# Per-head sums of squares from two split products, placed later in the tensor engine's order

## The chip, the cores and the metric

The kernel runs on one core of a Trainium2 chip. A core has five engines with their own instruction streams: TensorE (PE, with its weight loads shown apart as PEld), VectorE (DVE), ScalarE (ACT), GpSimd (POOL) and SyncE (SP), which here issues nearly all DMAs. Engines wait for one another through semaphores. The metric is the device time of one execution in microseconds (us).

## The reference

One step of a decoder trunk: one layer, 2048 prompt positions and 8 sample positions of width 1024 (32-bit floats). What bears on the change is the normalisation of q and k. Each has 12 heads of 64 in three groups of four (g = 0, 1, 2), and every head is divided by its own root mean square before the rotary turn's result is used:

```python
def rmsnorm(x, gain):
    xf = x.astype(jnp.float32)
    y = xf * lax.rsqrt(jnp.mean(xf * xf, axis=-1, keepdims=True) + EPS)
    return (y * gain.astype(jnp.float32)).astype(x.dtype)

def project_inputs(h, pos, w_in, q_norm_g, k_norm_g):
    z = h @ w_in
    u, q, k, v, a_pool, a_attn = jnp.split(z, IN_SPLITS, axis=-1)
    q = rope(rmsnorm(q.reshape(b, l, N_HEADS, HEAD_DIM), q_norm_g), pos)
    k = rope(rmsnorm(k.reshape(b, l, N_HEADS, HEAD_DIM), k_norm_g), pos)
    ...
```

Around it stand the modulated input norm, pooled and gated branches, dilated attention in the three head groups, an output projection, and a feed-forward part of width 4096 with squared relu.

## The kernel before

**Arithmetic.** Large products are made from 32-bit values split in two parts of the type float32r: the high part is a copy into that type (`S.copy`, ACT), the low part the difference (POOL for weights, L184). `mm3` (L156) makes three products of one block: high by high, high by low, low by high. One product of a 128x128 block with 512 columns in float32r is one instruction. `small` (L168) makes a single product of plain 32-bit floats: one instruction with two records, since it appears twice in the trace.

**Stages.** Up to 76 us the conditioning and the first normalised input; 76 to 298 us q, k and v of the first half of the positions (`qkv(0)`); 298 to 760 gates, conditioning and the pooled branch; 760 to 1128 q, k, v of the second half (`qkv(1)`), with batches of the attention (`ps_s`, `ps_t`, `ps_o`) laid between; then the rest of the attention, the output projection and the feed-forward part up to 3065 us. In each `qkv`, the head groups follow as g = 2, 1, 0, in each group q, then k, then v.

**Units.** q and k are made in units of at most 512 positions: 512, 256 and 264 (256 and the 8 sample positions) in `qkv(0)`, 512 and 512 in `qkv(1)`. There are 3 x 2 x 3 = 18 units in the first and 3 x 2 x 2 = 12 in the second, 30 in all: 18 of 512, 6 of 256, 6 of 264 columns. A unit has two halves of the head width (48 products of `ps_qk`). `qk_out` takes them out of PSUM on ACT as `ab` and, squared, as `qsq` (L381, L382). `after_qk` (L391) does the rest: it loads cosines and sines (`cs`, SP L395), adds the two squares on POOL (L396), does the rotary turn on DVE and POOL into `ro` (L400 to L405), and gives up its turn. Later it is called again: one `small` product with a matrix of ones per head (`hones`, part of the constants `cp`) sums the squares over the partitions of each head, into `ps_hs` (L408); ACT takes the root (L410), DVE the reciprocal (L411) and multiplies (L413); ACT and POOL split the result into `ohl` (L435, L436), and SP stores it as `qst` or `kst` (L444, L447).

**What sets the order.** TensorE's order is written out: the class `Order` adds up a model time from a length given with each product, and polls waiting generators after every third product. A generator yields the model time after which it is to go on; `after_qk` yields `HS_AT` there, 6500 model ns after the unit's products. So a greater number puts the `ps_hs` product later among the others. The order of all other engines is the scheduler's, which prefers what is under `first()`. All loads and stores of these stages stand in one queue, SP's, in that order, and one that waits holds those behind it. Weights come by `load_w` (L178), three raw buffers `wr`, one load ahead.

**Buffers.** In `gtp` there is a tag `th` with two buffers of 512 columns of 4 bytes, which `gate` uses from 298 us on.

Of the kernel before, what the change touches and what calls it, by code (L numbers as in the profile page):

```python
# [8 lines left out]
F32 = mybir.dt.float32  # L9
F32R = mybir.dt.float32r  # L10
# [6 lines left out]
P = 128  # L17
# [9 lines left out]
KEEP = (128, 512, 2048)  # L27
NEG = -1.0e30
DEPTH = 1
HS_AT = 6500  # L30
ADA_GAP = 3600
DEPTH_O = 1
R1 = 2
# [16 lines left out]
PERIOD1 = 4200.0  # L50
PERIOD2 = 3600.0
PRIO = 400
CPACK = (("cT", (8, 9)), ("bada", (48,)), ("gn", (2, 8)), ("ident", (128,)), ("ones", (128,)), ("hones", (128,)),
         ("mask", (256,)), ("qkg", (2, 2)), ("psc", (4,)), ("icnt", (4, 16)), ("stT", (4, 8, 15)), ("fold", (9,)),
         ("sel", (16,)), ("par", (2,)))
CPW = sum(int(np.prod(s)) for _, s in CPACK)
# [58 lines left out]
def emit(tc, I, O):  # L115
# [52 lines left out]
    def small(ps, w, x, ns=220.0):  # L168
        mm(ps, w, x, True, True, ns)
# [59 lines left out]
    for name, shape in CPACK:  # L229
# [5 lines left out]
            v = v.rearrange("p (a b c) -> p a b c", a=shape[0], b=shape[1])  # L235
        cv[name] = v
        off += n
    cT, ident, ones, hones, mask = cv["cT"], cv["ident"], cv["ones"], cv["hones"], cv["mask"]
    bada, gn, qkg, icnt, stT = cv["bada"], cv["gn"], cv["qkg"], cv["icnt"], cv["stT"]
    epsc = cst.tile([P, 1], F32, name="epsc")  # L240
    V.memset(epsc, EPS)
    mod = cst.tile([P, 48, 9], F32, name="mod")
# [141 lines left out]
    def qkv(ci, hb, done=None):  # L384
# [6 lines left out]
        def after_qk(g, qk, t0, n, ab, sq):  # L391
# [2 lines left out]
            cs = ap.tile([P, 2, 512], F32, tag="cs", bufs=2 - ci, name="cs")  # L394
            SP.dma_start(out=cs[:, :, :n], in_=I["rope"][:, :, BASE[ci] - 1024 * ci + t0:BASE[ci] - 1024 * ci + t0 + n])  # L395
            G.tensor_tensor(out=sq[:, 0, :n], in0=sq[:, 0, :n], in1=sq[:, 1, :n], op=ALU.add)  # L396
            a, b, co, si = ab[:, 0, :n], ab[:, 1, :n], cs[:, 0, :n], cs[:, 1, :n]
            t = ap.tile([P, 2, 512], F32, tag="rt", bufs=1, name="rt")
            o = ap.tile([P, 2, 512], F32, tag="ro", bufs=2, name="ro")
# [5 lines left out]
            V.tensor_tensor(out=o[:, 1, :n], in0=o[:, 1, :n], in1=t[:, 1, :n], op=ALU.add)  # L405
            yield HS_AT
            pst = stp.tile([P, 512], F32, tag="st", name="ps_hs")
            small(pst[:, :n], hones, sq[:, 0, :n], n / 0.6)  # L408
            rs = ap.tile([P, 512], F32, tag="qrs", bufs=2 - ci, name="qrs")
            S.activation(out=rs[:, :n], in_=pst[:, :n], func=AF.Sqrt, scale=1.0 / 64, bias=epsc)  # L410
            V.reciprocal(out=rs[:, :n], in_=rs[:, :n])  # L411
# [309 lines left out]
    def ada_load(op, b):  # L721
        out = []
        for kk in range(4):
            raw = op.tile([P, 1024], F32, tag="wr", bufs=8, name="wr")
            SP.dma_start(out=raw, in_=I["w_ada"][b, kk])
            out += [raw[:, 0:512], raw[:, 512:1024]]
        return out
# [10 lines left out]
    def opening():  # L738

        ost = ExitStack()  # L740
        op = pool(ost, "open", side="left")
        raws = {0: ada_load(op, 0)}
        x0 = load_x0(op, 0)
        raws[2] = ada_load(op, 2)
        raws[1] = ada_load(op, 1)
        keys = [("w_in", 8 + 6 * qk + i) for qk in range(2) for i in range(2)]
        ws, pss = [weights(*keys[0])], []
        x1 = load_x0(op, 1)
        raws[3] = ada_load(op, 3)
        hxs = hx(h0, KD, 0, 512)  # L750

        def part(t):
            if t:
                ws.append(weights(*keys[t]))
            pss.append(mmp.tile([P, 512], F32, tag="mm", name="ps_qk"))
            mm3(pss[t], wk(ws[t], KD)[:4], hxs[:4], False, stop=False)

        m0 = ada_rows(op, 0, raws[0])
        acc = x_sum(0, 0, x0, V)
        rs0 = rms_finish(npl, stp, acc, HALVES[0][0][2])  # L760
        m0()
        m2 = ada_rows(op, 2, raws[2])
        m2()
        make_h(0, 0, x0, rs0, h0, range(4))
        m1 = ada_rows(op, 1, raws[1])
        acc = x_sum(0, 1, x1, V)
        part(0)
        m1()
        part(1)
        m3 = ada_rows(op, 3, raws[3])  # L770
        rs1 = rms_finish(op, stp, acc, HALVES[0][1][2])
        part(2)
        m3()
        make_h(0, 0, x0, rs0, h0, range(4, KD))
        make_h(0, 1, x1, rs1, h0)
        part(3)
        ost.close()
        return ws, pss
# [689 lines left out]
```

## Time and profile before

| | us |
|---|---|
| median of three runs | 3069.55 |
| lowest, highest | 3059.91, 3071.53 |
| profiled execution, its own time | 3066.39 |
| its span in the trace | 3064.6 |

In that execution the granted TensorE clock was 0.98 of full speed on the mean. Busy shares of the span: PE 96%, PEld 82%, DVE 52%, ACT 32%, POOL 32%. The chain that ended last runs over PE for 76% of the span, over DVE for 5% and over DMAs for 5%. Times in the rows further down are microseconds from the start of the span; the second number of a row in a timeline is how long the group of instructions in it took, and square brackets hold idle time before it and what ended it. A product's record and its end are modelled, so neighbouring records overlap; the distance between starts is the safer number.

### The profile page before, as it was taken

To read this page: it belongs to the slowest core of one execution; us is meant where nothing else is said; L and a number is where in the kernel's file an instruction comes from. 1 tells how busy PE (TensorE), PEld (TensorE's weight loads), DVE (VectorE), ACT (ScalarE), POOL (GpSimd) and SP (SyncE) were. 2 spreads that over 40 slices of the span, in tenths; PEclk is the share of its full clock that TensorE was granted. 3 is DMA by queue.
4 is the path that set the end of the run, shared out by engine and by line. 5 is a ranking of instruction groups with operands and counts; after the bars stand their busy time and mean duration, and the time that the engine had idled before them with its cause. 6 is when DMAs were issued, how large, how long until landed. Compare 5 with 4: busy or idle time off the path is not lost.

```text
span 3064.6 us, 40910 instructions
## 1 busy us (share of the span) xinstructions
PE 2953.0 (96%) x16220; PEld 2516.0 (82%) x16220; DVE 1589.7 (52%) x2645; ACT 983.2 (32%) x1771; POOL 969.5 (32%) x510
## 2 busy tenths in 40 slices
PE   7999999999898789999999999999999999999999
PEld 3899788887788688877899999999877888888887
DVE  4656352541744524447865545555677554444444
ACT  4433342433554434433521221121235211111211
POOL 2666341333533312234532122121245312221221
PEclk8999999999999889999999999999999999999999
DMA  6453852334777779976321111111272211111111
GB/s 239 147 162 133 287 185 95 118 118 147 199 198 209 185 177 233 246 233 224 104 86 42 49 49 49 42 49 48 91 242 83 76 42 56 48 49 42 55 43 69
DMA packets 207599, 379.09 MB, mean 124 GB/s; under 512 B 47424, under 2 KB 103072, under 8 KB 206624
## 3 DMA queue, kind: packets, MB, share of 16 engines
q1 hardware_dynamic: 195888, 359.63, 38.3%
q10 hardware_dynamic: 11520, 16.85, 1.5%
q8 instruction: 128, 2.10, 0.3%
q14 instruction: 63, 0.52, 0.1%
HBM read 294.89 MB, written 81.75 MB: 123 GB/s over the span
## 4 chain that ended last, share of the span: by engine, by line
PE 76%; DVE 5%; DMA 5%; issue 4%; POOL 3%; ACT 2%; SPq 1%; DVEq 0%; ACTq 0%; POOLq 0%
PE ps_dn L153 23%; PE ps_up L153 22%; PE ps_g L153 10%; PE ps_v L153 4%; PE ps_qk L153 4%; PE ps_u L153 3%; PE ps_wo L153 3%; PE ps_o L153 2%; PE ps_pb L153 1%; POOL wh L184 1%; PE ps_s L153 1%; PE ps_ada L153 1%; PE ps_t L172 1%; DMA t1d<-ta 1%; POOL ohl L436 1%
## 5 line engine op out<-in xcount | busy, mean ns | idle before, releaser
L184 POOL TENSOR_TENSOR wh<-wr,wh 128x1024 fp32r<-128x1024 f32 (+1 forms) x274 | 651.0, 2384 | 1676.7 <-ACT wh L183 1668.5
L153 PE MATMUL ps_dn<-rt,wh 128*128 128x512 f32 (+2 forms) x3840 | 727.5, 350 | 5.5 <-POOL wh L184 3.3
L153 PEld LDWEIGHTS ps_dn<-rt,wh 128*128 128x128 f32 x3840 | 619.6, 188 | 108.8 <-POOL wh L184 4.2
L183 ACT CAST wh<-wr 128x1024 fp32r<-128x1024 f32 (+1 forms) x306 | 309.3, 1023 | 735.7 <-issue 562.3
L1293 DVE SCALAR_TENSOR_TENSOR xa<-ps_dn,mod,xa 128x512 f32<-128x512 f32 (+1 forms) x640 | 405.0, 641 | 202.9 <-PE ps_dn L153 201.5
L153 PE MATMUL ps_g<-h,wh 128*128 128x512 f32 (+2 forms) x1920 | 391.5, 355 | 0.4 <-POOL wh L184 0.4
L153 PE MATMUL ps_up<-hb,wh 128*128 128x264 f32 (+2 forms) x2304 | 371.5, 319 | 0.0
L153 PE MATMUL ps_up<-ha,wh 128*128 128x512 f32 x1536 | 365.7, 394 | 0.0
L153 PEld LDWEIGHTS ps_up<-hb,wh 128*128 128x128 f32 x2304 | 332.0, 188 | 36.3
L153 PEld LDWEIGHTS ps_g<-h,wh 128*128 128x128 f32 x1920 | 308.7, 191 | 48.5 <-POOL wh L184 1.0
L153 PEld LDWEIGHTS ps_up<-ha,wh 128*128 128x128 f32 x1536 | 286.7, 188 | 64.6 <-issue 0.5
L153 PE MATMUL ps_qk<-h,wh 128*128 128x512 f32 (+2 forms) x1440 | 301.5, 363 | 8.8 <-POOL h L318 6.5
L1277 DVE TENSOR_TENSOR r<-r 128x512 f32<-128x512 f32 (+2 forms) x160 | 99.2, 620 | 387.5 <-ACT r L1276 387.4
L153 PEld LDWEIGHTS ps_qk<-h,wh 128*128 128x128 f32 x1440 | 234.4, 193 | 51.0 <-POOL h L318 7.7
L1279 DVE TENSOR_TENSOR rt<-r,rt 128x512 fp32r<-128x512 f32 (+2 forms) x160 | 217.9, 1362 | 81.8 <-ACT rt L1278 81.6
L1276 ACT ACTIVATE r<-ps_up 128x512 f32<-128x512 f32 (+2 forms) x160 | 82.2, 514 | 415.1 <-PE ps_up L153 415.1
L153 PE MATMUL ps_v<-wh,h 128*128 128x256 f32 (+1 forms) x1224 | 171.8, 297 | 25.8 <-ACT wh L183 18.9
L153 PEld LDWEIGHTS ps_v<-wh,h 128*128 128x128 f32 (+1 forms) x1224 | 157.7, 195 | 31.1 <-ACT wh L183 19.3
L932 ACT ACTIVATE pe<-pe,ost 128x128 f32<-128x128 f32 (+1 forms) x192 | 87.1, 455 | 142.0 <-DVE ost L930 136.9
L930 DVE CUSTOM_DVE_ANT_0 pe<-ps_s,cp 128x128 f32<-128x128 f32 (+1 forms) x192 | 61.4, 358 | 119.6 <-PE ps_s L153 119.4
L1278 ACT CAST rt<-r 128x512 fp32r<-128x512 f32 (+2 forms) x160 | 85.8, 536 | 66.3 <-DVE r L1277 66.3
L436 POOL TENSOR_TENSOR ohl<-ro,ohl 128x256 fp32r<-128x256 f32 (+1 forms) x66 | 76.7, 1185 | 90.9 <-ACT ohl L435 90.8
(181 smaller groups left out, 3003.7 us busy)
## 6 DMA issues: line engine op xcount, KB each, us to landing
wr<-in_w_up SPq DMA_DIRECT2D x72, 512.0 KB
wr<-in_w_down SPq DMA_DIRECT2D x68, 512.0 KB
wr<-in_w_in SPq DMA_DIRECT2D x64, 512.0 KB
wr<-in_w_ada SPq DMA_DIRECT2D x48, 512.0 KB
slab<-kst SPq DMA_DIRECT2D x40, 512.0 KB
wr<-in_w_out SPq DMA_DIRECT2D x32, 512.0 KB
cs<-in_rope SPq DMA_DIRECT2D x18, 512.0 KB
qst<-ohl SPq DMA_DIRECT2D x9, 1024.0 KB
```

What stands on the lines that cost most here:

```text
L153: PE.matmul(ps, w, x, start=start, stop=stop)
L172: PE.transpose(ps, x, idn)
L183: S.copy(out=wt[:, 0, :n], in_=raw[:, :n])
L184: eng.tensor_tensor(out=wt[:, 1, :n], in0=raw[:, :n], in1=wt[:, 0, :n].bitcast(F32), op=ALU.subtract)
L436: G.tensor_tensor(out=pl, in0=pi, in1=ph.bitcast(F32), op=ALU.subtract)
L930: V.tensor_tensor_reduce(out=pe[:, off:off + nk], in0=ps[:, off:off + nk], in1=mask[:, mo:mo + nk], scale=-0.125, scalar=3.0e38, op0=ALU.a ...
L932: S.activation(out=pe[:, off:off + nk], in_=pe[:, off:off + nk], func=AF.Exp, scale=-1.0, bias=o[:, 64:65], accum_out=o[:, 65:66])
L1276: S.activation(out=r1[:, :l], in_=ps[:, :l], func=AF.Relu)
L1277: V.tensor_tensor(out=r1[:, :l], in0=r1[:, :l], in1=r1[:, :l], op=ALU.mult)
L1278: S.copy(out=rt[:, 0, a:a + l], in_=r1[:, :l])
L1279: V.tensor_tensor(out=rt[:, 1, a:a + l], in0=r1[:, :l], in1=rt[:, 0, a:a + l].bitcast(F32), op=ALU.subtract)
L1293: V.scalar_tensor_tensor(out=x[:, c0 + a:c0 + a + lp], in0=ps[:, :lp], scalar=mod[:, 40 + m, 0:1], in1=x[:, c0 + a:c0 + a + lp], op0=ALU.m ...
```

## The change

The matrix of ones per head leaves the packed constants (1355 to 1227 columns) and is loaded by itself in the opening, into one of the three raw buffers for weights, and copied on ACT to float32r. In each of the 30 units the sum of squares is split: a copy on ACT (`sh`) and a difference on DVE (`sl`), both under `first()`. They lie in the buffers of the tag `th`: a unit of 512 or 264 columns takes both, one of 256 takes one. The single product is replaced by two float32r products, and their model length is about 216 ns each for 512 columns in place of 853 in all. `HS_AT` goes from 6500 to 11000.

```diff
-HS_AT = 6500
+HS_AT = 11000
...
-CPACK = (("cT", (8, 9)), ("bada", (48,)), ("gn", (2, 8)), ("ident", (128,)), ("ones", (128,)), ("hones", (128,)),
+CPACK = (("cT", (8, 9)), ("bada", (48,)), ("gn", (2, 8)), ("ident", (128,)), ("ones", (128,)), 
...
-    cT, ident, ones, hones, mask = cv["cT"], cv["ident"], cv["ones"], cv["hones"], cv["mask"]
+    cT, ident, ones, mask = cv["cT"], cv["ident"], cv["ones"], cv["mask"]
...
+    hones = cst.tile([P, P], F32R, name="hones")
...
             G.tensor_tensor(out=sq[:, 0, :n], in0=sq[:, 0, :n], in1=sq[:, 1, :n], op=ALU.add)
+
+            m = 1 if n > 256 else 2
+            hl = [gtp.tile([P, m, 512 // m], F32R, tag="th", bufs=2, name="sqhl") for _ in range(2 // m)]
+            sh, sl = (hl[0][:, 0, :n], hl[-1][:, m - 1, :n])
+            with first():
+                S.copy(out=sh, in_=sq[:, 0, :n])
+                V.tensor_tensor(out=sl, in0=sq[:, 0, :n], in1=sh.bitcast(F32), op=ALU.subtract)
...
-            small(pst[:, :n], hones, sq[:, 0, :n], n / 0.6)
+            mm(pst[:, :n], hones, sh, True, False, max(107.0, n / 2.4 + 2.5))
+            mm(pst[:, :n], hones, sl, False, True, max(107.0, n / 2.4 + 2.5))
...
         raws[3] = ada_load(op, 3)
+        raw = rawp.tile([P, 1024], F32, tag="wr", name="wr")
+        SP.dma_start(out=raw[:, :P], in_=I["hones"])
+        S.copy(out=hones, in_=raw[:, :P])
```

TensorE in `qkv(0)`, the q units of group g = 1, named A (512), B (256) and C (264) below. Before:

```order
L153 MATMUL ps_qk<-h,wh 128x264 x12
L153 MATMUL ps_hs<-qsq,cp 128x512
L153 MATMUL ps_qk<-h,wh 128x264 x36
L153 MATMUL ps_qk<-h,wh 128x512 x3
L153 MATMUL ps_hs<-qsq,cp 128x256
L153 MATMUL ps_qk<-h,wh 128x512 x27
L153 MATMUL ps_hs<-qsq,cp 128x264
L153 MATMUL ps_qk<-h,wh 128x512 x18
```

And after:

```order
L153 MATMUL ps_qk<-h,wh 128x264 x48
L153 MATMUL ps_qk<-h,wh 128x512 x3
L153 MATMUL ps_hs<-sqhl,hones 128x512 x2
L153 MATMUL ps_qk<-h,wh 128x512 x21
L153 MATMUL ps_hs<-sqhl,hones 128x256 x2
L153 MATMUL ps_qk<-h,wh 128x512 x24
L153 MATMUL ps_hs<-sqhl,hones 128x264 x2
L153 MATMUL ps_qk<-h,wh 128x256 x48
```

Each `ps_hs` stands some 40 products later, and 24 products lie between that of B and that of C where 27 lay before. For the k units it is 45 products of 256 columns (`ps_v`).

DVE at the same place; `qrs` is the root that is inverted. Before:

```order
L404 TENSOR_TENSOR ro<-ro,rt 128x512
L405 TENSOR_TENSOR ro<-ro,rt 128x512
L401 TENSOR_TENSOR ro<-ab,cs 128x256
L403 TENSOR_TENSOR ro<-ab,cs 128x256
L404 TENSOR_TENSOR ro<-ro,rt 128x256
L405 TENSOR_TENSOR ro<-ro,rt 128x256
L411 RECIPROCAL qrs<-qrs 128x512
L413 TENSOR_TENSOR ro<-ro,qrs 128x512 x2
```

And after:

```order
L404 TENSOR_TENSOR sqhl<-qsq,sqhl 128x512
L409 TENSOR_TENSOR ro<-ab,cs 128x256
L411 TENSOR_TENSOR ro<-ab,cs 128x256
L412 TENSOR_TENSOR ro<-ro,rt 128x256
L413 TENSOR_TENSOR ro<-ro,rt 128x256
L404 TENSOR_TENSOR sqhl<-qsq,sqhl 128x256
L420 RECIPROCAL qrs<-qrs 128x512
L404 TENSOR_TENSOR sqhl<-qsq,sqhl 128x264
L422 TENSOR_TENSOR ro<-ro,qrs 128x512 x2
```

The difference of C (264 columns) stands behind the reciprocal of A. On ACT the copies of B and C both stand ahead of A's root, as the rows there after the change show:

```order
L183 CAST wh<-wr 128x1024
L403 CAST sqhl<-qsq 128x256
L403 CAST sqhl<-qsq 128x264
L419 ACTIVATE qrs<-ps_hs,epsc 128x512
L382 ACTIVATE ab<-ps_qk,cp 128x512
L383 ACTIVATE qsq<-ps_qk 128x512
L419 ACTIVATE qrs<-ps_hs,epsc 128x256
```

So A's root waits until C's copy has its buffer.

SP's queue near the end of `qkv(1)`, around the load of the last half of v's weights (`in_w_v`); `kst` there is the store of the first k unit of g = 0, and the `cs` load beside it belongs to the second. Before:

```order
L976 DMA att_79<-ost 128x4x66 x4
L968 DMA vt<-vscr 128x8x256
L395 DMA cs<-in_rope 128x2x512
L447 DMA kst_74<-ohl 512x1x512
L180 DMA wr<-in_w_v 128x1024
L180 DMA wr<-in_w_in 128x1024 x4
```

And after:

```order
L988 DMA att_79<-ost 128x4x66 x3
L456 DMA kst_74<-ohl 512x1x512
L988 DMA att_79<-ost 128x4x66
L980 DMA vt<-vscr 128x8x256
L396 DMA cs<-in_rope 128x2x512
L180 DMA wr<-in_w_v 128x1024
```

The store now stands ahead of the last attention store and of the `vt` load; the weight load is still behind both the store and the `cs` load.

## Rows read from the trace of the kernel before

**Rows 1.** The page's busy times: engine, us, share, instructions.

```profile
PE 2953.0 (96%) x16220; PEld 2516.0 (82%) x16220; DVE 1589.7 (52%) x2645; ACT 983.2 (32%) x1771; POOL 969.5 (32%) x510
```

**Rows 2.** Stretches: start:end, length; busy PE, PEld, DVE, ACT, POOL; granted clock, DMA.

```profile
76.00:150.00 74.00, 67.04 (x471) 62.34 (x471) 48.68 (x71) 31.51 (x61) 42.83 (x39) 0.95 0.44 142
150.00:298.00 148.00, 147.50 (x1033) 135.20 (x1032) 86.35 (x110) 53.46 (x97) 93.00 (x74) 1.00 0.46 150
1055.00:1072.00 17.00, 0.46 (x4) 0.26 (x3) 11.04 (x10) 3.62 (x11) 8.55 (x6) 0.65 0.57 186
1072.00:1084.00 12.00, 10.28 (x45) 9.98 (x46) 1.36 (x9) 2.73 (x10) 4.68 (x2) 0.50 0.62 180
```

**Rows 3.** Waits of PE, 70 to 300 us: total us, times, longest.

```profile
PE ps_hs L153 <- POOL qsq L396: 3.4, 3, 2.5
```

**Rows 4.** Waits of PE, 755 to 1130 us.

```profile
PE ps_v L153 <- ACT wh L183: 18.9, 2, 16.6
PE ps_o L153 <- ACT px L940: 5.7, 2, 3.7
```

**Rows 5.** The tile ps_hs: ns shortest/median/longest, first and last start, forms.

```profile
L153 PE MATMUL ps_hs<-qsq,cp x60: 377/591/697, 88.1 to 1084.8; 128*128 128x512 f32 x36, 128*128 128x256 f32 x12, 128*128 128x264 f32 x12
```

**Rows 6.** Weight loads around a 512-column product: start, us, instruction.

```profile
242.05 0.31 PEld L153 LDWEIGHTS ps_hs<-qsq,cp 128*128 128x128 f32 x2
242.59 0.19 PEld L153 LDWEIGHTS ps_qk<-h,wh 128*128 128x128 f32 x1 [0.24 <-issue]
243.02 0.56 PEld L153 LDWEIGHTS ps_qk<-h,wh 128*128 128x128 f32 x4 [0.24 <-issue]
```

**Rows 7.** Weight loads around a 256-column product.

```profile
105.60 0.30 PEld L153 LDWEIGHTS ps_hs<-qsq,cp 128*128 128x128 f32 x2
105.93 0.76 PEld L153 LDWEIGHTS ps_qk<-h,wh 128*128 128x128 f32 x5
```

**Rows 8.** Long runs of float32r products on PE.

```profile
981.55 8.58 PE L153 MATMUL ps_qk<-h,wh 128*128 128x512 f32 x36
204.97 15.48 PE L153 MATMUL ps_v<-wh,h 128*128 128x256 f32 x129
```

**Rows 9.** PE in the first units, where it waits.

```profile
88.14 1.12 PE L153 MATMUL ps_hs<-qsq,cp 128*128 128x512 f32 x2 [0.60 <-POOL qsq L396]
...
93.96 5.59 PE L153 MATMUL ps_qk<-h,wh 128*128 128x256 f32 x32 [3.86 <-POOL h L318]
...
127.50 0.71 PE L153 MATMUL ps_hs<-qsq,cp 128*128 128x264 f32 x2 [2.49 <-POOL qsq L396]
```

**Rows 10.** DVE in the units of g = 1.

```profile
162.48 1.76 DVE L404 TENSOR_TENSOR ro<-ro,rt 128x512 f32<-128x512 f32 x1 [1.18 <-POOL rt L400]
164.17 0.68 DVE L405 TENSOR_TENSOR ro<-ro,rt 128x512 f32<-128x512 f32 x1
164.77 0.41 DVE L401 TENSOR_TENSOR ro<-ab,cs 128x256 f32<-128x256 f32 x1
...
168.58 3.35 DVE L411 RECIPROCAL qrs<-qrs 128x512 f32<-128x512 f32 x1 [0.22 <-ACT qrs L410]
```

**Rows 11.** POOL at the same place.

```profile
162.40 1.29 POOL L396 TENSOR_TENSOR qsq<-qsq 128x512 f32<-128x512 f32 x1
...
171.14 2.39 POOL L184 TENSOR_TENSOR wh<-wr,wh 128x1024 fp32r<-128x1024 f32 x1 [0.40 <-ACT wh L183]
```

**Rows 12.** ACT: a copy out of PSUM of 264 columns, and a root.

```profile
107.28 0.48 ACT L381 ACTIVATE ab<-ps_qk,cp 128x264 f32<-128x264 f32 x1
...
167.85 0.69 ACT L410 ACTIVATE qrs<-ps_hs,epsc 128x512 f32<-128x512 f32 x1 [1.58 <-PE ps_hs L153]
```

**Rows 13.** SP's queue before the weight load of 1064 us.

```profile
1058.36 0.57 SPq L395 DMA_DIRECT2D cs<-in_rope  x1
1063.37 0.57 SPq L447 DMA_DIRECT2D kst<-ohl  x1
1063.99 0.62 SPq L180 DMA_DIRECT2D wr<-in_w_v  x1
```

## The prediction

> **What bounds the kernel now.** I read the busy times first: PE is busy for 96% of the span and no other engine for more than 52% [rows 1]. So the question for each edit is whether it changes what PE does, or what PE waits for. Then the stretches: between 76 and 150 us PE is busy for 67.04 of 74 us, between 150 and 298 us for 147.50 of 148 [rows 2]. The first half's q, k and v are bound by PE with next to nothing to spare; a new wait there is paid in full. Then the waits of PE there: for the sum of squares (POOL's addition) it waits three times, 3.4 us in all [rows 3]. In the second half's q, k and v the one large wait is for a weight of v, 16.6 us [rows 4], with the granted clock at 0.65 in that gap and at 0.50, the lower of its two levels, in the 12 us behind it [rows 2]. The changed products themselves are 30 of plain 32-bit floats (60 records) from 88 to 1085 us [rows 5]; nothing of the change is later than that, so everything must be won or lost in 1000 of 3065 us.
>
> **What a product costs.** I take the weight loads, whose starts are sharper than the modelled ends. Around a product of 512 columns two records start at 242.05, the next product's load at 242.59, the one behind that at 243.02 [rows 6]: from the first to the last 0.97 us hold the product and one spacing. One spacing is 0.12 us, from a run of 129 products of 256 columns in 15.48 us [rows 8]; off the 0.97 it leaves 0.85 for 512 columns. For 256 the first load stands 0.33 before the next product's [rows 7], and and the five loads behind it come every 0.14 us ((0.76 - 0.19) / 4) in place of 0.12, some 0.08 more in all: 0.41. The pair that replaces it costs two ordinary products: 36 of 512 columns take 8.58 us, 0.238 each [rows 8], so 0.48 a pair; of 256 columns 0.24. Saved: 0.37 for each of 512 columns and 0.17 for each of 256 or 264.
>
> The Trainium skill (FP8 and Floating Point Precision, TensorE Precision Notes) says that a true 32-bit product takes four passes through the array. By that, four times 0.238 is 0.95 and 0.47 would be saved for 512 columns, so that the second half's 12 units would win 5.6 us in place of the 4.4 that the row gives.
>
> **The sum for PE.** Second half: 12 x 0.37 = 4.4. First half: 6 units of 512 columns and 12 shorter ones. The very first product ran in front of a wait that PE had anyway (3.86 us for the input's low part, at 93.96 [rows 9]), so its time was free, and since it moves later, behind that wait, its 0.48 now counts: 5 x 0.37 + 12 x 0.17 - 0.48 = 3.4. PE gains 7.8.
>
> **Waits that go.** A later place takes away PE's wait for POOL at 127.50 (2.49 us) and one of 0.32; the third, 0.60 at 88.14, lay in the shadow named above [rows 3, 9]. That is 2.8, if nothing else is late there. What is late next is the copy and the difference that now stand between the addition and the product.
>
> **The new chain.** Each unit has a copy on ACT and a difference on DVE more. For 512 columns a similar instruction takes 0.69 on ACT [rows 12] and on DVE 0.68 alone (L405) but 1.76 where it began beside POOL's addition (L404, at 162.48) [rows 10, 11]. For a shorter unit 0.48 and 0.41. Thirty of them are 16 to 21 us of ACT and 17 to 43 of DVE over 600 us, and neither engine is full there; what counts is only the time at which the products come. Since A and C take both buffers, the copy of the next unit waits until the product of the last one is done. Between A and B that is harmless: 0.48 + 0.41 against 21 products of 0.238 = 5.0 us. Between B and C the order is against it: C's copy waits for B's product; A's root stands behind that copy on ACT; A's reciprocal waits for the root; C's difference stands behind the reciprocal on DVE; C's product waits for the difference. With 0.48 + 0.69 + 3.35 + 0.43 [rows 10, 12] and about 0.3 for four hand-overs (the 0.22 before the reciprocal is one such row) that is 5.2 us. TensorE has 24 x 0.238 = 5.7 us of work there for q and 45 x 0.120 = 5.4 for k. For k two copies of v out of PSUM can stand in DVE's way as well, some 0.4 each: 6.0 against 5.4. This happens in g = 1 and g = 0, so four times: 0, 0.6, 0, 0.6. In g = 2 the units follow each other with a margin of 0 to 2 us that I cannot read closer than that. I put 2 us on all new waits of the first half. The lower end is 0; the upper is 17 (each product but the first 1 us late, the difference between 0.68 and 1.76).
>
> The rows say that a DVE operation with two inputs in SBUF that begins 0.08 us after POOL's starts ends 0.55 us after POOL's does, and takes 1.76 in place of 0.68 [rows 10, 11]. The Trainium skill (SBUF, SBUF: two separate sides) tells of an exclusive lock between the two, held for a whole instruction, and the one that comes second is blocked; the trace agrees, since 1.76 is about the 1.21 left of POOL's 1.29 and then 0.68. By that rule a difference that meets a weight's low part on POOL can lose up to 2.39 us, and with all four long chains hit the sum would be some 8 us worse; the sum here takes one hit in two, within the 2 us above.
>
> **The second half beside PE's own time.** Here the copies and differences stand among the attention's maxima, exponentials and copies, and PE waits for those in places (5.7 us for `px` [rows 4]). 12 x (0.69 + 0.68) = 16 us of instructions, most of them beside PE's products: I take 1.5 us; the ends are 0 and 12 x (0.69 + 1.76) = 29.
>
> The 16.6 us wait is the weight load issued at 1063.99 behind a `cs` load at 1058.36 and a store at 1063.37 in SP's queue [rows 13]. In the new order the store comes first, then an attention store, the `vt` load, `cs`, and the weight, still behind both. The store now needs a product that is put 4.5 us of model time later; the `cs` load then no longer holds it. I take -1, between -22 (the whole wait goes, and with it 6 us lost to half the clock over 12 us [rows 2]) and +5 (the store comes later by that much and the load with it). In g = 1 the same kind of wait, 2.3 us of the 18.9 [rows 4], I take as unchanged but for 1 us more, which cancels the -1.
>
> **The opening.** One more raw buffer is in use, so the third weight load waits for the first weight's low part; that weight is needed much later, and the loads' wait is hidden by the conditioning rows. Cost 0; without that cover it would be 2.39, one weight's low part on POOL [rows 11].
>
> **Sum.** -7.8 - 2.8 + 2 + 1.5 - 1 + 1 = -7.1. The profiled execution's own time of 3066.39 becomes 3059.3; that execution lies 3.2 under the median of 3069.55, so for a median I say 3062.
>
> **Rivals.**
> - *The stall goes.* The weight of v gets out of SP's queue in time, as the store that stood in front of it is put ahead of two other transfers. For it: the `kst` store no longer stands directly in front. Against it: `cs`, which waits for the rotary turn, still does. Then -16.6 and -6 more: about 3040.
> - *The new waits eat the gain.* Eight of the 17 products wait 1 us or somewhat less for a difference held by POOL or by a reciprocal. For it: margins under 1 us in four places, and a busy share of PE that leaves no slack [rows 2]. Against: 24 to 48 products lie between most of them. -7.1 + 8: about 3070.
> - *Slower.* In the second half, ACT's copy waits for POOL's addition or for the buffer, and the attention's exponentials queue behind it; DVE's difference waits for the copy, with the attention's maxima behind it. At 0.69 + 1.76 for 12 units, all on PE's path, +29 - 8: about 3090. It decides from 8 us of such waiting upward. For: both are preferred by `first()` as they are emitted, ahead of work that is ready. Against: ACT and DVE are each half idle there, and most attention batches have other products beside them.
> - *It doesn't do what it says.* From the old product's first load to the next product's it is only 0.54 us [rows 6]. If that were its whole price, about that of two ordinary products (0.48), and the gap behind it another load's, the pair would save almost nothing and only waits would change: 3068 to 3070. Against it: the same 0.24 gap stands before both loads behind the product.
>
> **How the numbers follow.** Half a per cent, 15 us, is about what a measurement tells from no change here, so the borders are 3054 and 3085. Forecast 0.52, with its own range 3053 to 3069; the stall goes 0.13; gain eaten 0.17; slower 0.10; product no cheaper 0.08. Faster by over 0.5%: the stall's 0.13 and a sixth of the forecast's, 0.22. Slower: 0.08, as a fifth of the slower case stays under 3085. The rest, 0.70, is no change. The range leaves out a part of the stall's case and the slower one: 3044 to 3078.
>
> **What would show it.** Right: PEld's starts around `ps_hs` 0.48 apart in place of 0.85 to 0.97; no PE wait for POOL's `qsq`; at most four waits for DVE's `sqhl`, none over 1 us, all before C's product; the wait for v's weight still near 16 us. Wrong: waits of over 1 us in a row of units; more waits for `px` or `pe` in the attention; the wait for v's weight gone or moved, or the low clock in another place. A different span beyond 1130 us would be something I have not thought of.

## The result, and the profile after

The changed kernel takes 3096.95 us (median; lowest 3090.76, highest 3104.27) against 3068.03 us for the kernel before, both measured anew: a ratio of 1.0102, interval 1.0086 to 1.0118. It is about 29 us slower, where 3062 was forecast. The profiled execution took 3091.71 us, with a span of 3089.9, 25.3 more than before.

The busy times of the changed kernel, the line that answers to [rows 1]:

```profile
PE 2944.6 (95%) x16220; PEld 2514.4 (81%) x16220; DVE 1610.0 (52%) x2675; ACT 996.6 (32%) x1802; POOL 965.2 (31%) x510
```

PE is busy for 8.4 us less than before: the cheaper product is there. But the span grew by 25.3, so PE waits or runs slowly for some 34 us more. The weight loads around the first product of A in g = 1 (start, us, instruction), the answer to [rows 6]:

```profile
167.12 0.42 PEld L153 LDWEIGHTS ps_hs<-sqhl,hones 128*128 128x128 f32 x2
167.59 1.58 PEld L153 LDWEIGHTS ps_qk<-h,wh 128*128 128x128 f32 x7
```

From the pair's first load to the next product's it is 0.47 us, where 0.48 was forecast. Before, these two stood 0.54 apart, and the load behind them came another 0.43 later: 0.97 in all [rows 6].

Where the time goes I read by boundaries that all traces have: the start of the last or first product of a kind. The stages end with the last `ps_v` of the first half, the last `ps_pb`, the last `ps_qk` of g = 2 in the second half, the last `ps_v`, the first `ps_wo`, and the end. The first column is the length before, the others the difference to it, in us; e5 and e6 have the change in one half alone; they and the other runs are told of further down.

| stage, to | before | after | e5 first half | e6 second half | e15 place only | e16 split only | e9 | e14 | e18 |
|---|---|---|---|---|---|---|---|---|---|
| last v, first half | 298.2 | +0.3 | +9.2 | -3.0 | -0.4 | -1.7 | +7.6 | -2.4 | -0.3 |
| last pooled product | 449.2 | +1.2 | +2.9 | +4.2 | +0.6 | 0.0 | +2.5 | +0.5 | +2.6 |
| q, k of g = 2, second half | 65.6 | +9.6 | +0.4 | +7.1 | +5.4 | +3.4 | -2.4 | +1.4 | +1.0 |
| last v | 315.2 | -0.7 | -1.1 | -1.5 | +1.5 | -10.8 | +8.3 | -21.5 | -0.4 |
| first output product | 257.7 | +13.2 | +2.2 | +13.1 | +12.2 | +19.2 | +16.4 | +12.8 | -1.4 |
| end | 1678.7 | +1.7 | +0.3 | +0.7 | 0.0 | +4.5 | +6.9 | -2.8 | -2.0 |

One execution each, so a few us either way in a cell are chance. In the changed kernel two stages carry the loss: q and k of g = 2 in the second half, and the stretch after the last v, in which TensorE has the same products to do as before, bar four of `ps_o`. The first half looks untouched in this execution; others show it slower (below).

**First half.** PE's waits from 70 to 298.5 us after the change (total us, times, longest), the answer to [rows 3]:

```profile
PE ps_v L153 <- POOL wh L184: 5.6, 2, 3.1
PE ps_qk L153 <- POOL h L319: 3.7, 1, 3.7
PE ps_qk L153 <- POOL wh L184: 1.8, 1, 1.8
PE ps_hs L153 <- DVE sqhl L404: 1.5, 1, 1.5
PE ps_qk L153 <- ACT h L318: 1.4, 1, 1.4
PE ps_v L153 <- ACT wh L183: 1.0, 1, 1.0
```

The wait for `qsq` is gone and only one for the difference (1.5) is new, as forecast. What was not forecast is the first, third and last row: 8.4 us of waits for weights, of which 0.2 were there before. At the end of g = 1's q and k, PE is 7.0 us ahead of the kernel before (190.0 against 197.0); at the end of its v it is 1.2 ahead. The weight's chain at that place on ACT:

```profile
190.35 1.21 ACT L444 CAST ohl<-ro 128x256 fp32r<-128x256 f32 x2 [2.50 <-DMA qst<-ohl]
191.47 0.48 ACT L382 ACTIVATE ab<-ps_qk,cp 128x264 f32<-128x264 f32 x1
191.84 0.38 ACT L383 ACTIVATE qsq<-ps_qk 128x264 f32<-128x264 f32 x1
192.11 1.05 ACT L183 CAST wh<-wr 128x1024 fp32r<-128x1024 f32 x1
```

and on POOL:

```profile
192.81 1.67 POOL L445 TENSOR_TENSOR ohl<-ro,ohl 128x256 fp32r<-128x256 f32 x2
194.44 2.34 POOL L184 TENSOR_TENSOR wh<-wr,wh 128x1024 fp32r<-128x1024 f32 x1
```

The weight's low part ends at 196.78, and PE goes on at 196.84. Before, the low part ended at 199.54. ACT and POOL, working through the units in their order, are thus 2.8 us earlier with this weight than before; PE is 7.0 us earlier and waits.

**Second half, q and k of g = 2.** PE's waits there after the change, 749.1 to 824.5 us; before, the last was 0.4 and the first was not there:

```profile
PE ps_t L172 <- ACT pe L944: 4.9, 1, 4.9
PE ps_o L153 <- ACT px L952: 4.1, 1, 4.1
PE ps_o L153 <- DVE ost L962: 3.3, 1, 3.3
```

The last of them on DVE (L942 is the attention's maximum, L962 its copy out of PSUM):

```profile
780.83 3.35 DVE L420 RECIPROCAL qrs<-qrs 128x512 f32<-128x512 f32 x1 [3.34 <-ACT qrs L419]
784.10 0.23 DVE L942 CUSTOM_DVE_ANT_0 pe<-ps_s,cp 128x128 f32<-128x128 f32 x1
...
784.25 3.03 DVE L422 TENSOR_TENSOR ro<-ro,qrs 128x512 f32<-128x512 f32 x2
787.20 0.28 DVE L942 CUSTOM_DVE_ANT_0 pe<-ps_s,cp 128x128 f32<-128x128 f32 x1
...
787.41 2.63 DVE L404 TENSOR_TENSOR sqhl<-qsq,sqhl 128x512 fp32r<-128x512 f32 x1
789.97 0.28 DVE L942 CUSTOM_DVE_ANT_0 pe<-ps_s,cp 128x128 f32<-128x128 f32 x1
...
790.17 0.41 DVE L962 COPY ost<-ps_o 128x256 f32<-128x256 f32 x1
```

and on POOL, beside the difference at 787.41:

```profile
786.69 2.81 POOL L184 TENSOR_TENSOR wh<-wr,wh 128x1024 fp32r<-128x1024 f32 x1
```

PE waits for the copy at 790.17. In front of it stand a reciprocal, two multiplications and the new difference, 9.0 us of DVE's time. Before, the same reciprocal and multiplications ran from 775.96 to 780.66. Now they come five microseconds later, and the attention's maxima and copy stand between and behind them. The wait of 4.9 us is alike, with a rotary turn (L409 to L413, 811.08 to 818.97) and the multiplications ahead of the maximum at 818.90.

**After the last v.** PE's waits from 1138.7 to 1409 us after the change:

```profile
PE ps_s L153 <- DMA slab<-kst: 6.5, 1, 6.5
PE ps_g L153 <- POOL wh L184: 3.2, 3, 1.7
PE ps_ab L153 <- POOL wh L184: 2.2, 2, 1.9
PE ps_ab L153 <- DMA ay<-ayd: 1.9, 1, 1.9
PE ps_y L172 <- DVE y L1096: 1.7, 1, 1.7
```

and in the same stretch before (1128.3 to 1385 us):

```profile
PE ps_s L153 <- DMA slab<-kst: 4.3, 1, 4.3
PE ps_ab L153 <- ACT wh L183: 2.3, 2, 1.8
PE ps_ab L153 <- POOL wh L184: 1.6, 2, 1.0
PE ps_g L153 <- POOL wh L184: 0.4, 1, 0.4
PE ps_ab L153 <- DMA ay<-ayd: 0.4, 1, 0.4
```

No single wait explains 13 us; most rows of before are a little longer, and new ones stand beside them.

### The profile page after: what moved, and what is told of

Same layout as the page of the kernel before. It is cut to its first block, busy times and chain, and to the rows that moved or that the text cites. A ratio compares the mean times of both kernels' runs of the same rounds, so it can differ in the third digit from the quotient of the medians.

```text
span 3089.9 us, 40948 instructions
## 1 busy us (share of the span) xinstructions
PE 2944.6 (95%) x16220; PEld 2514.4 (81%) x16220; DVE 1610.0 (52%) x2675; ACT 996.6 (32%) x1802; POOL 965.2 (31%) x510
## 4 chain that ended last, share of the span: by engine, by line
PE 71%; DVE 7%; DMA 4%; issue 3%; POOL 3%; ACT 2%; SPq 1%; DVEq 0%; ACTq 0%; POOLq 0%
PE ps_dn L153 22%; PE ps_up L153 22%; PE ps_g L153 9%; PE ps_qk L153 3%; PE ps_u L153 3%; PE ps_wo L153 3%; PE ps_v L153 2%; PE ps_o L153 2%; PE ps_s L153 1%; PE ps_pb L153 1%; POOL wh L184 1%; PE ps_ada L153 1%; PE ps_t L172 1%; DMA slab<-kst 1%; DMA cs<-in_rope 1%
## 5 line engine op out<-in xcount | busy, mean ns | idle before, releaser
L153 PE MATMUL ps_qk<-h,wh 128*128 128x512 f32 (+2 forms) x1440 | 299.9, 362 | 12.2 <-POOL h L319 6.4
L942 DVE CUSTOM_DVE_ANT_0 pe<-ps_s,cp 128x128 f32<-128x128 f32 (+1 forms) x192 | 61.8, 359 | 100.2 <-PE ps_s L153 94.9
```

Of the source, the lines that this page charges most:

```text
L153: PE.matmul(ps, w, x, start=start, stop=stop)
L942: V.tensor_tensor_reduce(out=pe[:, off:off + nk], in0=ps[:, off:off + nk], in1=mask[:, mo:mo + nk], scale=-0.125, scalar=3.0e38, op0=ALU.a ...
```

## The experiments

Each ratio is to the kernel before on the same chip, with its 95% interval.

**Place or split, in both halves (e1, e2).** The theories named in the expectations: the split's own instructions hold ACT and DVE (1), the later place drops root, reciprocal and multiplications among the attention's work (2), any new order does it (3).

```diff
 # e1: the kernel before
-HS_AT = 6500
+HS_AT = 11000
 # e2: the changed kernel
-HS_AT = 11000
+HS_AT = 6500
```

> The kernel before with HS_AT at 11000 and nothing else. Theory 1 (the added copy and difference, put ahead of ready work, hold the attention's maxima and copies on DVE and ACT in the second half): the extra work is absent, so 3060 to 3070 us, no 3.3 us wait of TensorE for DVE's ost copy near 790 us. Theory 2 (the later place of the product moves root, reciprocal and the two multiplications into the stretch where the attention's maxima are due): 3085 to 3100 us, with such waits of over 3 us in the first attention batches. Theory 3 (any new order moves the stalls of the second half about): anything from 3050 to 3100, with stalls in other places.

Measured: 3088.38 us, 1.006 (1.0037 to 1.0083).

> The changed kernel with HS_AT back at 6500: the split products in the old place. Theory 1: 3085 to 3100 us, the waits for DVE and ACT in the second half stay, and in the first half TensorE waits for the difference before many products, since less lies between. Theory 2: 3060 to 3070 us in the second half, plus 5 to 15 us of waits for the difference in the first half. Theory 3: no number.

Measured: 3086.15 us, 1.006 (1.0041 to 1.008). Either part alone costs about 20 us; neither theory 1 nor 2 alone holds. But e2 does more than put the split back: the pair's model length is 432 ns in place of 853, so the model time, which also places the attention's batches, runs differently from that of the kernel before (more on this below).

**Is it the added instructions, or their priority? (e3, e4)**

```diff
 # e3: squares in a float32r tile; POOL writes the sum in float32r;
 #     the low part is left out and the sum doubled
-            G.tensor_tensor(out=sq[:, 0, :n], in0=sq[:, 0, :n], in1=sq[:, 1, :n], op=ALU.add)
+            G.tensor_tensor(out=sh, in0=sq[:, 0, :n].bitcast(F32), in1=sq[:, 1, :n].bitcast(F32), op=ALU.add)
-                S.copy(out=sh, in_=sq[:, 0, :n])
-                V.tensor_tensor(out=sl, in0=sq[:, 0, :n], in1=sh.bitcast(F32), op=ALU.subtract)
...
-            mm(pst[:, :n], hones, sl, False, True, max(107.0, n / 2.4 + 2.5))
+            mm(pst[:, :n], hones, sh, False, True, max(107.0, n / 2.4 + 2.5))
 # e4: the changed kernel, copy and difference as they are, but not under it
-            with first():
```

> The changed kernel without the split: the sum of squares is written by POOL in float32r and multiplied twice as it is (the low part left out, the sum doubled). TensorE's work and places stay as in the changed kernel; the 30 copies on ACT and 30 differences on DVE and the wait for their buffers are gone. Theory 1: 3055 to 3065 us. Theory 2: 3085 to 3095 us, as in the changed kernel less a few us. Theory 3: no number.

Measured: 3093.71 us, 1.0086 (1.0067 to 1.0106).

> The changed kernel with the copy and the difference outside of first(), so that the scheduler puts them by their own priority. Theory 1: the attention's maxima are less often held, 3070 to 3085 us, with some waits of TensorE for the difference before the product. Theory 2: 3090 to 3100 us, no better. Theory 3: no number.

Measured: 3096.78 us, 1.0094 (1.0075 to 1.0113). TensorE's order is that of the changed kernel in both. Without copies and differences the loss is all but the same. So theory 1 isn't what makes the changed kernel slow, nor is the mechanism of the forecast's slower rival.

**Which half, and is it any change of order? (e5 to e8)**

```diff
 # e5, e6: new = ci == 0, or new = ci == 1; the constant in both float32r and, by bitcast, plain
+            if new: (the split)
-            yield HS_AT
+            yield HS_AT if new else 6500
 # e7, e8: the kernel before
-HS_AT = 6500
+HS_AT = 6000   (e8: 7000)
```

> Split products and 11000 in the first half's 18 units alone; the 12 units of the second half have the full-precision product at 6500. Theory A (the loss comes from the second half's order): 3060 to 3072 us; in the first half TensorE is 5 to 7 us early after g = 1's q and k and has lost it by 298 us, since the chain of the single ohl buffer (copy, POOL, store, next copy) holds the next weights. Theory B (any change of order makes the scheduler's order of the attention worse): 3080 to 3095 us too.

Measured: 3076.96 us, 1.003 (1.0017 to 1.0043).

> Split products and 11000 in the second half's 12 units alone; the first half as before. Theory A: 3088 to 3100 us, the whole loss. Theory B: 3080 to 3095 us.

Measured: 3085.81 us, 1.0063 (1.0047 to 1.0079).

> The kernel before with HS_AT at 6000 in place of 6500 and nothing else, a control: every product as it was, a few places in TensorE's order moved by three to six products. Theory A (the later place costs, since roots, reciprocals and multiplications fall among the attention's): 3060 to 3075 us. Theory B (any change of order costs): 3080 to 3095 us.

Measured: 3068.34 us, 1.0003 (0.9993 to 1.0013).

> The kernel before with HS_AT at 7000, the control on the other side. Theory A: 3065 to 3075 us, a small step of the 20 us that 11000 cost. Theory B: 3080 to 3095 us.

Measured: 3065.17 us, 0.9995 (0.9985 to 1.0006). The halves add up (0.30% and 0.63% against 1.02%), and both cost: e5 lies between the ranges of theories A and B, e6 in B's. The controls e7 and e8 cost nothing, so theory 3 (B in these expectations) falls as it stood. e7 moves the sums of squares alone. e8 also moves the attention's products on TensorE, by up to 18 products of q, k, v and the gates, mostly to an earlier place; its stages change (5.5 us more for q and k of g = 2, 12.9 less up to the last v, 8.7 more behind it), its time does not. The first half's part is larger than the changed kernel's profile shows: the last v product starts at 298.5, 307.4, 302.4, 305.8, 306.1 and 305.0 us in the six profiles with the changed first half (after, e5, e13, e9, e11, e17), at 294.7 to 298.2 in six with that of before (before, e6, e10, e14, e15, e16). The late weights don't need the split's instructions: with the place alone (e1) or without copies and differences (e3), TensorE waits 4.4 and 8.0 us for weights in the first half, and the last v product starts at 298.1 and 297.5. In e5, PE's stop for the weights is followed by a stretch at a lower granted clock, 0.72 in these 12 us (start:end, length, busy PE, PEld, DVE, ACT, POOL, clock):

```profile
200.00:212.00 12.00, 10.14 (x63) 9.99 (x64) 8.51 (x11) 1.68 (x5) 5.70 (x4) 0.72 0.40 115
```

So the gain in front of a late weight can be paid back twice: as the wait, and at the lower clock behind it.

**The attention's work put first (e9, e10).** Here theory A says that the moved product's followers on DVE and ACT hold the attention's work; the order of TensorE stays as it is.

```diff
+            with first():
                 V.tensor_tensor_reduce(out=pe[:, off:off + nk], in0=ps[:, off:off + nk], ...)
                 S.activation(out=pe[:, off:off + nk], in_=pe[:, off:off + nk], func=AF.Exp, ...)
...
+        with first():
             S.copy(out=px[:, :off], in_=pt[:, :off])
...
+        with first():
             V.tensor_copy(out=ost[:, u0:u0 + nu, 0:64], ...)
```

> The changed kernel with the attention's maxima, exponentials and copies out of PSUM under first() too, so that the scheduler no longer puts roots, reciprocals, multiplications and rotary turns ahead of them. Theory A (the later product drops its followers on DVE and ACT among the attention's, and TensorE waits for those): the waits for pe, px and ost in the second half fall from 25 us to under 12, and 3065 to 3080 us. Rival (those waits come from PE's own order, not from what stands ahead on DVE and ACT): 3088 to 3100 us, waits as they were.

Measured: 3101.51 us, 1.0112 (1.0091 to 1.0133).

> The kernel before with the same preference for the attention's instructions, the control of the run above. Theory A: little to win, since only 15 us of such waits are there: 3055 to 3070 us. Rival: 3065 to 3075 us.

Measured: 3073.96 us, 1.0021 (1.0009 to 1.0034). e10 is a little slower than before, outside theory A's 3055 to 3070 and inside its rival's 3065 to 3075. In e9 the stage of q and k of g = 2 is repaired, 63.2 us against 75.2 after and 65.6 before; PE's waits there:

```profile
PE ps_o L153 <- ACT px L954: 3.8, 1, 3.8
PE ps_s L153 <- DMA slab<-kst: 0.5, 1, 0.5
PE ps_o L153 <- DVE ost L965: 0.3, 1, 0.3
```

That shows the mechanism at its place: with the attention ahead of the root's followers, and TensorE's order untouched, the waits for `pe` and `ost` are gone. In the whole second half the waits for `pe`, `px` and `ost` fall from 25.4 to 8.7 us, as theory A had it. But the time did not follow. The next stage is 9 us longer than in the changed kernel: where that had waits for v's weights of

```profile
PE ps_v L153 <- ACT wh L183: 25.5, 2, 18.7
PE ps_v L153 <- POOL wh L184: 5.8, 2, 3.1
```

and next to none of q and k for theirs or for `vt`, e9 has

```profile
PE ps_v L153 <- ACT wh L183: 25.1, 2, 18.7
PE ps_v L153 <- POOL wh L184: 9.0, 2, 5.8
PE ps_qk L153 <- POOL wh L184: 4.2, 1, 4.2
PE ps_qk L153 <- DVE vt L510: 4.1, 1, 4.1
```

and the whole is no faster. ACT and DVE are half idle on the mean there, POOL two thirds, and still putting one kind of work first made another late.

**First half: the buffer or the loads' distance? (e11, e12, e17)**

```diff
 # e11 on e5, e12 on the kernel before
-            ohl = ap.tile([P, 2048], F32R, tag="ohl", bufs=1, name="ohl")
+            ohl = ap.tile([P, 2048], F32R, tag="ohl", bufs=2 - ci, name="ohl")
 # e17 on e5
+    depth[0] = 2
     qkv(0, h0)
+    depth[0] = DEPTH
```

> The change in the first half alone, with two ohl buffers there in place of one. Theory C (the chain copy, POOL, store, next copy of the single buffer holds ACT, the weights' copies stand behind it, and TensorE's gain of 5 to 7 us is lost to waits for weights): the waits for wh in the first half, 8.6 us, go to under 3 and the time falls to 3060 to 3068 us. Rival (POOL is short of time as such in that stretch): waits for wh stay over 5 us, 3072 to 3080 us.

Measured: 3077.76 us, 1.0027 (1.0013 to 1.0042); 8.4 us of waits for weights remain, as many as in e5.

> The kernel before with two ohl buffers in the first half, the control. Theory C: TensorE does not wait for weights there before, so 3063 to 3070 us. Rival: the same.

Measured: 3072.59 us, 1.0018 (1.0003 to 1.0033), with longer waits for `qsq` in the first half, 8.1 us in place of 3.4.

> The change in the first half alone, with weights loaded two ahead there. If the late weights that meet TensorE's gain are a matter of the loads' distance: waits for wh from 8.6 us to under 3, and 3060 to 3068 us. If of ACT's and POOL's own order and time: the waits stay over 6 us, 3072 to 3080 us.

Measured: 3079.3 us, 1.004 (1.0026 to 1.0055); 7.0 us of waits for weights remain, 6.6 of them for the low part on POOL. Theory C falls: neither the second buffer nor the earlier load helps. What is late, by the rows, is the split of the weight on ACT and POOL, behind the units' own work; no run put that split first, so this is read and not tested.

**Second half: weights two ahead (e13, e14).**

```diff
+    depth[0] = 2
     qkv(1, h1[0], group_done)
...
         gate(1, h1[0], 16, m, t1d, mmp, lambda: next(fac))
+    depth[0] = DEPTH
```

> The changed kernel with weights loaded two ahead in place of one from the second half's q, k and v to the end of its gates. Theory E (in the stretch after v the loss is weights that come late, since each load stands in SP's queue behind stores that wait for TensorE's own products): the waits for wh after v go from 6.5 us to under 2, the stretch from the last product of v to the output projection falls from 271 to 258 to 262 us; the 25 us of waits for v's weights go under 10; 3060 to 3080 us in all. Rival (the late weights follow from a DMA load at its limit): the stretch stays at 268 us or more, 3085 to 3100 us.

Measured: 3085.82 us, 1.0069 (1.0054 to 1.0084).

> The kernel before with the same two loads ahead, the control. Theory E: the 18.9 us of waits for v's weights go under 8, little else changes, 3050 to 3068 us. Rival: 3062 to 3075 us.

Measured: 3057.84 us, 0.9981 (0.9971 to 0.9991): a version a little faster than both. Here the wait for v's weights that the forecast spoke of [rows 4, 13] is gone, and the stage ends 22 us earlier; but the stretch after it is 12.8 us longer. In e13 the late weights after v are gone too, and others stand in their place (1128.8 to 1397 us):

```profile
PE ps_y L172 <- DVE w L1084: 6.4, 1, 6.4
PE ps_y L172 <- DVE y L1096: 4.3, 3, 1.7
PE ps_s L153 <- DMA slab<-kst: 2.9, 1, 2.9
PE ps_ab L153 <- POOL wh L184: 1.2, 2, 0.6
```

The waits for `wh` fell to 2.3 us, close to what theory E had, but the stretch stayed at 268.6 us, as the rival had it. Theory E falls as the cause.

**Second half: place and split apart (e15, e16).**

```diff
 # e15: the kernel before
-            yield HS_AT
+            yield 11000 if ci else HS_AT
 # e16: e6 with
-            yield HS_AT if new else 6500
+            yield 6500
```

> The kernel before with 11000 in the second half's 12 units alone and the full-precision product. Theory A (the later place costs by what follows the product on ACT and DVE): 3080 to 3090 us, most of the 17 us of the second half. Rival (the split's own instructions cost): 3066 to 3074 us.

Measured: 3082.6 us, 1.0057 (1.0041 to 1.0073).

> The split products in the second half's 12 units alone, at 6500. Theory A: 3066 to 3075 us, the product's gain of some 4 us against waits for copy and difference. Rival (the split's own instructions cost): 3080 to 3090 us.

Measured: 3080.37 us, 1.0046 (1.0033 to 1.0059). The place alone gives most of e6's 1.0063, as theory A had it; the split alone nearly as much, as its rival had it; they do not add. Both lengthen the stretch after the last v (by 12.2 and 19.2 us), and in e15 the wait for `pe` of the first attention batches is there, 4.0 us. In e16 the 19.2 must be read with the 10.8 that the stage before it is shorter: 20 records of the attention's products move from the one to the other.

Neither run changes one thing alone. The attention's batches are placed by the same model time, and its products (`ps_s`, `ps_t`, `ps_o`) stand elsewhere on TensorE among the products of q, k, v and the gates than before: up to 6 products earlier to 18 later in e15, up to 54 later in e16 (whose pair is shorter in model time), up to 9 earlier to 39 later in the changed kernel and e6. So what e16 loses may come from the copies and differences or from that order; no run has the split with TensorE's order of before.

**The cheap product alone, in the old order (e18).**

```diff
 # e3 (no low part, the sum doubled) with
-HS_AT = 11000
+HS_AT = 6500
-            mm(pst[:, :n], hones, sh, True, False, max(107.0, n / 2.4 + 2.5))
-            mm(pst[:, :n], hones, sh, False, True, max(107.0, n / 2.4 + 2.5))
+            mm(pst[:, :n], hones, sh, True, False, n / 1.2)
+            mm(pst[:, :n], hones, sh, False, True, n / 1.2)
```

> TensorE's order of the kernel before, word for word, with the pair of float32r products in each full-precision product's place (model length as before, HS_AT 6500); the low part is left out and the sum doubled, so that no copy or difference is added. If the product's own saving counts: 7 to 9 us less work on TensorE, 3058 to 3064 us. If TensorE's time there is free anyway (waits behind it grow by what is saved): 3066 to 3072 us.

Measured: 3070.87 us, 1.0013 (1.0002 to 1.0024). TensorE's order is that of before, product for product. TensorE does less (its busy times first), and in the first half it waits longer for the sum of squares:

```profile
PE 2939.2 (96%) x16220; PEld 2510.5 (82%) x16220; DVE 1581.4 (52%) x2645; ACT 983.1 (32%) x1772; POOL 966.3 (32%) x510
```

```profile
PE ps_hs L153 <- POOL qsq L398: 7.4, 3, 5.8
```

3.4 before, 7.4 here. From the last `ps_qk` of g = 2 to the last v of the second half TensorE is idle for 46 us in place of 41, too. With the same products in the same order, what TensorE saves it waits longer for.

## Why the prediction was wrong, step by step

**The cost of the products: right.** 0.47 us a pair against a forecast of 0.48. e18, with the order of before, shows the saving: from a pair's first load to the ninth load behind the pair it takes 0.37 to 0.41 us less than with the old product for 512 columns and 0.18 to 0.22 less for the shorter ones, wherever TensorE does not wait. The forecast had 0.37 and 0.17. PE's busy time fell by 8.4 us in the changed kernel, where 7.8 was forecast.

**"The first half's q, k and v are bound by PE with next to nothing to spare": the step that failed first.** A busy share of 147.50 in 148 us [rows 2] says that PE did not wait; it does not say that the others had time in hand. The forecast then took PE's 7.8 us off the span. e18 shows that this gain, by itself, is worth nothing (1.0013): the sums came no sooner, and the waits grew. In the changed first half it is not zero but a loss: the forecast's terms for this half make 3.4 + 2.8 - 2, a gain of 4.2 us, and e5 is 0.30% slower, some 8 us. What stands there is 8.4 us of waits for weights, which no term of the sum held, and lower clock behind them.

**"Waits that go" and "the new chain": right in place, small in size.** The wait of 2.49 us for `qsq` went, and of the forecast's waits for the difference one came (1.5 us, for a difference of g = 2). The knife-edge chains of g = 1 and 0, put at 0.6 us twice, cost nothing.

**"I take 1.5 us" for the second half: the step that failed by most.** Its upper end was 29, and 17 to 20 us is what the half costs (1.0063). The term counted the added copies and differences. It did not count what follows the moved product on other engines: root, reciprocal (3.35), two multiplications (1.28 before, 3.03 here), the low part, the store. Only in SP's queue did the forecast follow what the moved step issues. e15, with no copy or difference, shows that the later place, with what it moves of the attention's order, is enough for most of the loss. e9 shows how it works in q and k of g = 2, where the changed kernel loses 9.6 us. The greater part, 13.2 us, lies in the stretch after the last v; what causes it there stays open (below).

**The wait for v's weight: right in the main.** It stayed (18.7 us against 16.6), behind both transfers in SP's queue. The same kind of wait in g = 1, put at 1 us more, grew from 2.3 to 6.7. The rival in which it goes happened in e14, from another edit.

**The rivals.** "Slower", about 3090, was given 0.10 and came nearest in time, but that is luck: its mechanism (the added instructions, preferred by `first()`) isn't needed, since e3 without them and e4 without the preference are as slow. "The gain is eaten" had the first half's direction with the wrong wait, the difference in place of the weight.

**The difference beside POOL.** The difference that began at 787.41, 0.72 us after a weight's low part on POOL, took 2.63 us where those of its size that meet no POOL instruction take 0.69, and ended 0.54 us after POOL did (789.50); one maximum behind it stood the copy that PE waits for. The Trainium skill (SBUF, SBUF: two separate sides) tells of an exclusive lock by which the one that comes second is blocked; the trace agrees. The forecast had priced that for the four long chains of the first half, and there it did not strike: C's differences of g = 1 and 0 took 0.37 to 0.43. It struck others: one of g = 2, which began beside a weight's low part at 114.14, took 1.73, and PE waited 1.5 for it.

**Open.** The stretch after the last v is 11 to 23 us longer in every kernel with a changed second half, whether by place, split or weights two ahead (8.7 in e8), and within 3 us of before in e5, e7, e10, e11, e12, e17 and e18. Its waits change from kernel to kernel (weights, the merge's `w` and `y` on DVE, slabs), and TensorE's idle time in it is 19 to 25 us in place of 11. Three things could cause it. One is TensorE's own order of the attention's products, which the edits move as told above; but e14 has TensorE's order of before, product for product, and its stretch is 12.8 us longer, so a moved order is not needed for it. Another is that the stage before ends earlier and leaves more to wait for; that fits e14, e8, e2 and e16, but in the changed kernel, e6 and e15 that stage is as long as before, within 2 us. The third is the order that the scheduler makes there for the other engines: DVE's is that of before, instruction for instruction, in e5, e7, e11, e12, e17 and e18, and another in every kernel with the longer stretch (and in e10, without one). That speaks for the third, but no run held those orders fixed, so it is argued and not shown.

## What to carry to other kernels

A busy share near 100% says that an engine does not wait, not that its work is worth its time: before pricing a saving, look at how late its suppliers are (here the weight's low part ended at 199.54 before, and PE began on it at 199.59). When an instruction is moved, price the whole train behind it on the other engines, where it arrives now, and what it meets there. Ask, too, what else the edit moves: here the model time that places the product also places the attention's batches. And test a saving by itself in an unchanged order (as e18 does): that one run tells whether there is anything to win.

## What the runs showed of the hardware

After the change the granted clock was 0.64 in the 20 us with PE's wait for v's weight, and 0.50, the lower of its two levels, in the 8 us behind it.

```profile
1062.00:1082.00 20.00, 2.27 (x16) 1.93 (x14) 6.18 (x6) 2.94 (x6) 5.19 (x4) 0.64 0.79 229
1082.00:1090.00 8.00, 3.88 (x15) 3.59 (x16) 6.09 (x10) 3.61 (x5) 7.63 (x4) 0.50 0.33 126
```

Waits of 4.1 us in all, as in e5 up to 201.86, stood beside a clock of 0.72 from 200 to 212 us:

```profile
198.24 0.50 PE L153 MATMUL ps_v<-wh,h 128*128 128x256 f32 x2 [1.00 <-ACT wh L183]
201.86 3.14 PE L153 MATMUL ps_v<-wh,h 128*128 128x256 f32 x13 [3.12 <-POOL wh L184]
```

In the changed kernel's execution the same two waits came 5 us earlier, and the clock was 0.87 from 190 to 200 us and 0.97 from 200 to 212. What a stop of that length costs by the clock differs from one execution to another.
